# The second layer's norm and first value products beside the last accumulation; values, first gate tile, routing's transposes and level 0 moved by a chunk

## The chip, the cores and the metric

The kernel runs on one core of one Trainium2 chip. The metric is the device time of one execution in microseconds (us); the median of three runs of the kernel before is 2987.86 us (2985.18 to 2990.16).

## What is computed

A decoder trunk of two layers on 512 tokens of width 1024, in fp32:

```python
for i in range(DEPTH):                       # DEPTH = 2
    h = rmsnorm(x, norm_mix[i])
    proj = h @ w_in[i]                       # 1024 x 3088, split into three causal mixers
    o_da = diff_attention(q, k, v, ...)      # 4 heads
    o_sc = short_conv(sc_b, sc_c, sc_h, conv_w[i])
    o_g  = gla(g_q, g_k, g_v, log_a)         # gated linear attention, then norm and silu gate
    x = x + concat([o_da, o_sc, o_g]) @ w_out[i]
    x = x + peer(rmsnorm(x, norm_ffn[i]), w_q, keys1, keys2, u, v)   # 16384 experts, 8 heads, top 16
return rmsnorm(x, norm_final)
```

## The kernel before

Every product of two fp32 matrices is made of three matmuls on high and low parts (`mm3`: high by high, high by low, low by high, in the rows L79, L80 and L81). A part is split by a ScalarE cast (high) and a VectorE subtraction (low), in `split` (L84, L85) or in the like lines of the PEER stage.

A layer is one `mixer` and one `peer`. In `mixer`, the norm's generator `norm_T` takes the token blocks of 128 in the order 3, 0, 1, 2: normed rows on VectorE (L205), eight transposes on TensorE (psn, L209), high and low part out of PSUM (L211, L212). The columns of `w_in` come as slabs: `slab` loads four pieces of two k tiles (wraw, three buffers, L260) on the queue of SyncE (SP) and splits them. The first slab (column 2560) gives the values of the gated linear attention (psv), the next (column 2816, 272 wide) its output gate and low-rank decay (psp). Then `across` makes the other projections, and `fill` runs the generator `gla` between them up to a sum of costs; its first level (level 0) is the row pst (L589), which reads ks and qs from VectorE, and further on stand trk (transposes of kd) and psu.

`peer` treats all 16384 experts densely for tokens 0 to 383 (TD), in 128 chunks of 128 experts; tokens 384 to 511 get their 128 experts a token by indirect loads instead (`gathered`, side work on POOL and VectorE that `tick` hands out; it ends in yacc). For a chunk, `hidden` is 24 psh matmuls with the split u rows and a Gelu into ht; for the first 72 chunks (NPRE) ht is stored to H in DRAM. Meanwhile `routing` runs on VectorE: `route` makes the top 16 of a block and three transposes (rtr, L1109 to L1111) for one-hot lists, and `gate_matrix` turns them into one-hot rows (oha, ohb, ohh, ohl) and psg matmuls; the gates go to G in DRAM. After chunk 74 the second phase goes over the chunks, from 72 on and then 0 to 71: `w_hi` multiplies ht by the gate tile g, loaded from G for eight chunks at a time (`load_g`, L889), and casts it, `v_hi` casts the v rows (vraw, L884), `w_lo` and `v_lo` make the low parts, and `accumulate` is 18 pv matmuls into six PSUM banks. The last four chunks are accumulated as a group, block by block (`group`, 24 matmuls each of three blocks), and each block's x is added from PSUM (L1003), with its norm's factor made right after (`x_rstd`, L191, on ScalarE and small VectorE operations).

What sets the order: each engine runs its instructions in one order, SP's loads too. A scheduler sets it from the program's order and its own costs, except for instructions under `pin`/`keep_in_program_order`, which keep the program's. `issue_after` holds an instruction's place behind another. A tile waits for the readers of what had its memory before.

Of the kernel before, what the change touches and what calls it, by code (L numbers as in the profile page):

```python
# [7 lines left out]
F32 = mybir.dt.float32  # L8
F32R = mybir.dt.float32r
# [10 lines left out]
P = 128  # L20
# [47 lines left out]
class K:  # L68
# [152 lines left out]
    def mixer(self, L):  # L221
# [3 lines left out]
        with ExitStack() as mc:  # L225
# [3 lines left out]
            qT = mp.tile([P, 4, T], F32, name="qT")  # L229
            kT = mp.tile([P, 4, T], F32, name="kT")  # L230
            va = mp.tile([P, TB, T], F32, name="va")
            hh, hl = self.new_act()
            rows = lambda t: [t[:, 2 * i:2 * i + 2].rearrange("p a b -> p (a b)") for i in range(2)]
            norm = self.norm_T(ins["norm_mix"][L:L + 1, :], hh, hl, rows(va) + rows(kT), order=ORDER)
            with ExitStack() as wc:
                wp = wc.enter_context(tc.tile_pool(name="wpool", bufs=2, reuse_waits="tile"))
                qp = wc.enter_context(tc.tile_pool(name="qkn", bufs=2, reuse_waits="tile"))
# [56 lines left out]
                if L == 0:  # L294
                    self.constants(qT.rearrange("p a b -> p (a b)"), turn)
# [392 lines left out]
    def peer(self, L, xh, xl, rest):  # L688
# [3 lines left out]
        with ExitStack() as pc:  # L692
# [151 lines left out]
            ahead(0)  # L844
            best(NQ - 1)
            qc.close()
            with tc.tile_pool(name="route", bufs=1, reuse_waits="tile") as rp, tc.tile_pool(name="onehot", bufs=2, reuse_waits="tile") as hp:

                def routing():
                    for tb in range(TB):  # L850
                        if tb == ROUTE_AT:
                            yield from self.route(V12[3], I12[3], rp, gat, idx=idx, base=L * NCH * P)
                            yield None
                        if tb == TB - 1:
                            continue
                        gt = rp.tile([P, P], F32, tag="gt", name="gt")
                        yield from self.route(V12[tb], I12[tb], rp, gt, hk=(E1, E2, GH, GL), tb=tb)
                        for bt in range(P // TBAT):
                            yield from self.gate_matrix(tb * (P // TBAT) + bt, E1, E2, GH, GL, G, hp)

                work = routing()
                spent, live = 0.0, False
# [11 lines left out]
                for w in work:  # L874
                    print("leftover routing", w)
            lc.close()
            vp = pc.enter_context(tc.tile_pool(name="vstream", bufs=1, reuse_waits="tile"))
            late = vp
            pvs = [self.psA.tile([P, 512], F32, tag="a", name=f"pv{i}") for i in range(4)]
            pvs += [self.psC.tile([P, 512], F32, tag="c", name=f"pv{i}") for i in (4, 5)]  # L880
            order = list(range(NPRE, NCH)) + list(range(NPRE))
            def load_v(c):
                vs[c] = vp.tile([P, D], F32, tag="vraw", name="vraw", bufs=NVR)
                pin(nc.sync.dma_start(vs[c], ins["v_rows"][(L * NCH + c) * P:(L * NCH + c + 1) * P, :]))  # L884

            def load_g(c, h=None):
                if c // GE not in gt:
                    g = vp.tile([P, TD // TBAT, GE * TBAT], F32, tag="g", name="g", bufs=NG)
                    pin(nc.sync.dma_start(g, G[c // GE]))  # L889
                    gt[c // GE] = g  # L890
                if c < NPRE:
                    hs[c] = new_h() if h is None else h
                    pin(nc.sync.dma_start(hs[c], H[c]))

            vh, vl, wh, wl = {}, {}, {}, {}

# [21 lines left out]
                if i < NCH - NS:  # L918
                    f(order[i])

            ws, raws = [], {}

            def ahead_v(c):
                if not ws:
                    t = self.up.tile([P, 4, TD], F32R, tag="uwa", name="wsa", bufs=NUW // 2)
                    ws.extend([t[:, 0:2], t[:, 2:4], self.up.tile([P, 2, TD], F32R, tag="uraw", name="wsb", bufs=NUR)])
                t = self.up.tile([P, 2, D], F32R, tag="uwb" if len(raws) < 2 else "uwa", name="vs", bufs=NUW // 2)
                vh[c], vl[c] = t[:, 0], t[:, 1]
                t = ws.pop(0)
                wh[c], wl[c] = t[:, 0], t[:, 1]  # L930
                raws[c] = [self.up.tile([P, n], F32, tag="uraw", name=nm, bufs=NUR) for n, nm in ((D, "vr"), (TD, "hr"))]
# [32 lines left out]
            for i, c in enumerate(order):  # L964
                rate = RATE[1] if c >= NPRE else RATE[2]
                if i:
                    load_u(NPRE + i + LAG + 4)
                at(load_v, i + 3)
                at(load_g, i + 4)
                split_u(NPRE + i + LAG + 2)  # L970
                if i + LAG < NF:
                    hidden(order[i + LAG])
                tick(rate / 2)
                at(v_lo, i + 1)
                at(w_lo, i + 1)
                at(w_hi, i + 2)
                at(v_hi, i + 2)
                for k in range(NS):
                    j = NCH - 6 + 4 * (k - NS)
                    for step, f in ((j, ahead_v), (j + 2, ahead_hi), (j + 3, ahead_lo)):  # L980
                        if i == step:
                            f(order[NCH - NS + k])
                if i < NCH - NS - 1:
                    for tb in range(TD // P):
                        accumulate(tb, i)
                tick(rate / 2)
            for _ in side:
                pass
            nc.vector.tensor_tensor(self.x[:, 3], self.x[:, 3], yacc, op=OP.add)
# [4 lines left out]
            if last:  # L994
                fg = gp.tile([P, D], F32, tag="row", name="fg", bufs=NROW)
                nc.sync.dma_start(fg, ins["norm_final"].rearrange("(o d) -> o d", o=1).partition_broadcast(P))
                self.final(3, fg, gp)
            for tb in range(TD // P - last):
                for i in group:
                    accumulate(tb, i)  # L1000
# [3 lines left out]
                self.rstd[tb] = self.x_rstd(tb, sq)  # L1004
                if last:
                    self.final(tb, fg, gp)
            if last:
                tb = TD // P - 1
                y = gp.tile([P, D], F32, tag="row", name="fy", bufs=NROW)
# [28 lines left out]
    def route(self, V12, I12, rp, gate, hk=None, tb=0, idx=None, base=0):  # L1038
# [79 lines left out]
    def gate_matrix(self, bt, E1, E2, GH, GL, G, hp):  # L1118
        nc = self.nc
        stg = hp.tile([P, NCH, TBAT], F32, tag="stg", name="stg")  # L1120
        for o in range(TBAT // OHT):
# [10 lines left out]
            nc.vector.tensor_tensor(AH, A, tok(GH), op=OP.mult)  # L1132
            nc.vector.tensor_tensor(AL, A, tok(GL), op=OP.mult)
# [76 lines left out]
```

## Time and profile before

| | |
|---|---|
| median of three runs | 2987.86 us |
| profiled execution, its own time | 2988.17 us |
| its span, first to last instruction | 2986.4 us |
| VectorE busy | 80% |
| ScalarE busy | 42% |
| GpSimd (POOL) busy | 24% |
| DMA, mean over the span | 255 GB/s |

The span is what the trace holds; the profiled execution's own time is 1.8 us more. A row of the timeline gives start, duration, engine, line, operation and tiles; the bracket at its end is the engine's idle time before it and what ended it. `psn<-ident,kT` reads: the tile psn is written from ident and kT. PE is TensorE, PEld its weight loads, DVE VectorE, ACT ScalarE, SPq the issues of SyncE's queue.

### The profile page before, as it was taken

The page shows a single profiled execution, that of the slowest core. Times are in us where ns is not written, and L with a number is a line of the kernel's source. Part 1 is how long each engine was busy: PE and PEld are TensorE (multiplying, and loading weights), DVE is VectorE, ACT ScalarE, POOL GpSimd, SP SyncE. Part 2 cuts the span into 40 slices and gives each one's busy share as a digit, 9 for nine tenths or more (in the row PEclk, how much of TensorE's full clock was granted, in tenths as well). Part 3 has the DMA queues.
Part 4 walks back from the last instruction along what each step waited for, and adds up shares of the span by engine and source line. Part 5 has one row for each costly group of instructions (what it writes and reads, how often), then busy time and mean ns, then how long its engine had stood idle before and what let it go on. Part 6 is the DMA issues. An engine that isn't in the chain of part 4 may idle for free.

```text
span 2986.4 us, 44512 instructions
## 1 busy us (share of the span) xinstructions
PE 2937.2 (98%) x16262; PEld 2616.0 (88%) x16262; DVE 2393.9 (80%) x4754; ACT 1256.5 (42%) x1859; POOL 711.4 (24%) x617
## 2 busy tenths in 40 slices
PE   7999999999999999999989999999999999999998
PEld 6878899999899999888878688999999999988887
DVE  6676999976877788877866769999758777888778
ACT  5253355665333332333353433556553333323333
POOL 0200000222444455222102000012215444552220
PEclk9999999999999999999999999999999999999999
DMA  4322257999999998999543122579999999989995
GB/s 128 92 75 73 92 162 256 312 304 349 347 331 327 328 342 315 366 333 344 214 111 90 64 81 91 188 256 323 304 346 341 328 330 335 334 313 363 341 348 206
DMA packets 335867, 760.24 MB, mean 255 GB/s; under 512 B 30720, under 2 KB 191392, under 8 KB 331552
## 3 DMA queue, kind: packets, MB, share of 16 engines
q1 hardware_dynamic: 160656, 435.19, 40.8%
q0 software_dynamic: 75776, 271.62, 25.6%
q10 hardware_dynamic: 99216, 50.60, 5.6%
q8 instruction: 127, 2.08, 0.3%
q14 instruction: 92, 0.75, 0.1%
HBM read 673.15 MB, written 81.00 MB: 253 GB/s over the span
## 4 chain that ended last, share of the span: by engine, by line
PE 92%; DVE 4%; DMA 2%; ACT 1%; issue 1%; SPq 0%; ACTq 0%; DVEq 0%
PE pv L80 11%; PE pv L79 11%; PE pv L81 11%; PE psh L79 11%; PE psh L80 11%; PE psh L81 11%; PE psp L80 2%; PE psp L79 2%; PE psp L81 2%; PE psq L79 2%; PE psq L80 2%; PE psq L81 2%; PE psg L1139 2%; PE psg L1140 1%; PE pss L743 1%
## 5 line engine op out<-in xcount | busy, mean ns | idle before, releaser
L806 POOL DMA_INDIRECT row<-in_u_rows,idx x256 | 344.8, 1347 | 1358.7 <-DMA H<-ht 686.7
L79 PE MATMUL pv<-vh,wh 128*128 128x512 f32 x1500 | 583.0, 390 | 8.0 <-ACT vh L904 8.0
L80 PE MATMUL pv<-vl,wh 128*128 128x512 f32 x1500 | 584.7, 390 | 0.1
L81 PE MATMUL pv<-vh,wl 128*128 128x512 f32 x1500 | 583.8, 390 | 0.0
L806 POOL DMA_INDIRECT row<-in_v_rows,idx x256 | 315.3, 1232 | 597.4 <-DVE yacc L822 545.2
L724 ACT ACTIVATE ht<-psh 128x384 f32<-128x384 f32 x256 | 125.9, 492 | 775.7 <-PE psh L81 773.3
L899 DVE TENSOR_TENSOR vl<-vraw,vh 128x1024 fp32r<-128x1024 f32 x250 | 305.9, 1224 | 111.0 <-ACT vh L904 100.3
L79 PE MATMUL psh<-ahi,uwb 128*128 128x384 f32 x1024 | 348.2, 340 | 0.0
L79 PE MATMUL psh<-ahi,uwa 128*128 128x384 f32 x1024 | 346.4, 338 | 0.0
L80 PE MATMUL psh<-alo,uwb 128*128 128x384 f32 x1024 | 345.7, 338 | 0.0
L81 PE MATMUL psh<-ahi,uwb 128*128 128x384 f32 x1024 | 345.4, 337 | 0.0
L80 PE MATMUL psh<-alo,uwa 128*128 128x384 f32 x1024 | 344.2, 336 | 0.0
L81 PE MATMUL psh<-ahi,uwa 128*128 128x384 f32 x1024 | 344.1, 336 | 0.0
L79 PEld LDWEIGHTS pv<-vh,wh 128*128 128x128 f32 x1500 | 282.0, 188 | 63.2 <-ACT vh L904 8.6
L81 PEld LDWEIGHTS pv<-vh,wl 128*128 128x128 f32 x1500 | 282.3, 188 | 59.4 <-DVE wl L899 0.7
L80 PEld LDWEIGHTS pv<-vl,wh 128*128 128x128 f32 x1500 | 282.3, 188 | 56.0 <-DVE vl L899 1.6
L822 DVE SCALAR_TENSOR_TENSOR yacc<-row,wk,yacc 128x1024 f32<-128x1024 f32 x254 | 325.4, 1281 | 1.8
L912 ACT CAST wh<-ht 128x384 fp32r<-128x384 f32 x250 | 127.9, 512 | 432.8 <-DVE ht L1028 415.7
L813 DVE SCALAR_TENSOR_TENSOR row<-row,xg 128x1024 f32<-128x1024 f32 x256 | 308.7, 1221 | 0.0
L709 DVE TENSOR_TENSOR uwb<-uraw,uwb 128x1024 fp32r<-128x1024 f32 x144 | 176.0, 1222 | 123.3 <-ACT uwb L708 123.0
L709 DVE TENSOR_TENSOR uwa<-uraw,uwa 128x1024 fp32r<-128x1024 f32 x144 | 175.8, 1223 | 117.0 <-ACT uwa L708 116.8
L904 ACT CAST vh<-vraw 128x1024 fp32r<-128x1024 f32 x250 | 262.5, 1050 | 1.9 <-DMA vraw<-in_v_rows 1.9
(342 smaller groups left out, 5727.6 us busy)
## 6 DMA issues: line engine op xcount, KB each, us to landing
uraw<-in_peer_u SPq DMA_DIRECT2D x256, 512.0 KB, 5.4
vraw<-in_v_rows SPq DMA_DIRECT2D x250, 512.0 KB, 6.6
G<-stg ACTq DMA_DIRECT2D x48, 1024.0 KB, 7.5
g<-G SPq DMA_DIRECT2D x32, 1536.0 KB, 10.2
H<-ht SPq DMA_DIRECT2D x144, 192.0 KB, 4.8
ht<-H SPq DMA_DIRECT2D x138, 192.0 KB, 7.4
wraw<-in_w_in SPq DMA_DIRECT2D x88, 256.0 KB, 3.0
uraw<-in_peer_w_q SPq DMA_DIRECT2D x32, 512.0 KB, 3.4
```

The lines of the kernel that those rows point to most:

```text
L79: mm(ps, ah, bh, start=first, stop=False)
L80: mm(ps, ah, bl, start=False, stop=False)
L81: mm(ps, al, bh, start=False, stop=last)
L709: self.last = pin(nc.vector.tensor_tensor(lo, src, hi.bitcast(F32), op=OP.subtract))
L724: pin(nc.scalar.activation(hs[c], ps, AF.Gelu))
L806: nc.gpsimd.indirect_dma_start(out=r, out_offset=None, in_=ins[name], in_offset=bass.IndirectOffsetOnAxis(ap=idx[:, k:k + 1], axis=0))
L813: nc.vector.scalar_tensor_tensor(r, r, 1.0, xg, op0=OP.mult, op1=OP.mult, accum_out=hd[:, k:k + 1])
L822: nc.vector.scalar_tensor_tensor(yacc, r, wk[:, k:k + 1], yacc, op0=OP.mult, op1=OP.add)
L899: self.last = pin(nc.vector.tensor_tensor(lo, src, hi.bitcast(F32), op=OP.subtract))
L904: pin(nc.scalar.copy(vh[c], vs[c]))
L912: pin(nc.scalar.copy(wh[c], hs[c]))
L1139: nc.tensor.matmul(ps[:, j], B[at], AH[at], start=True, stop=False)
```

## The change

1. *Between the layers.* In layer 0's `peer`, the first slab of layer 1 (`first`) is loaded six chunks before the end, split before the last group, and `norm_T` of layer 1 runs between the group's blocks; the psv products follow in the same place (`values`), into PSUM tiles that layer 1's `mixer` copies out. Layer 0's own start stays.
2. *Level 0.* `fill(10)` is called after the first copy of the next projection, not ahead of it.
3. *Routing.* `route` and `gate_matrix` yield once more for the first block, and the loop leaves off for that chunk at such a yield: the transposes and the first one-hot row move back by a chunk.
4. *First values and gate tile.* The pool of the second phase is opened when routing ends; the first v load is issued in chunk 71's step and the first g load in chunk 72's, ahead of the remaining u loads.
5. The buffers of the last three chunks (`ahead_v`) are other ones: vraw, ht, g, uraw, uwa and xg in place of uwa, uwb and uraw. Not shown below.

```diff
-            hh, hl = self.new_act()
-            rows = lambda t: [t[:, 2 * i:2 * i + 2].rearrange("p a b -> p (a b)") for i in range(2)]
-            norm = self.norm_T(ins["norm_mix"][L:L + 1, :], hh, hl, rows(va) + rows(kT), order=ORDER)
+            if L == 0:
+                hh, hl = self.new_act()
+                rows = lambda t: [t[:, 2 * i:2 * i + 2].rearrange("p a b -> p (a b)") for i in range(2)]
+                norm = self.norm_T(ins["norm_mix"][L:L + 1, :], hh, hl, rows(va) + rows(kT), order=ORDER)
+            else:
+                hh, hl = self.hh, self.hl
...
-                next(norm)
-                wh, wl = slab(2560, 256)
+                if L == 0:
+                    next(norm)
+                    wh, wl = slab(2560, 256)
                 for i, tb in enumerate(ORDER):
-                    next(norm, None)
-                    ps = self.psC.tile([P, 256], F32, tag="c", name="psv")
-                    for k in range(KD):
-                        self.mm3(ps, hh[:, k, tb * P:tb * P + P], hl[:, k, tb * P:tb * P + P], wh[:, k], wl[:, k],
-                                 k == 0, k == KD - 1)
+                    if L:
+                        ps = self.psv.pop(tb)
+                    else:
+                        next(norm, None)
+                        ps = self.psC.tile([P, 256], F32, tag="c", name="psv")
...
-                fill(10)
...
                         nc.scalar.copy(dst[:, 2 * h + j], ps)
+                        if i == j == 0:
+                            fill(10)
...
-                for c in range(NPRE + LAG):
-                    if c:
-                        ahead(c)
-                    if live:
-                        tick(RATE[0])
-                    while spent < DVE_STEP * (c + 1):
-                        w = next(work, 1e9)
-                        if w is None:
-                            live = True
-                        else:
-                            spent += w
...
+            for c in range(NPRE + LAG):
+                if c:
+                    ahead(c)
+                if live:
+                    tick(RATE[0])
+                while vp is None and spent < DVE_STEP * (c + 1):
+                    w = next(work, Ellipsis)
+                    if w is Ellipsis:
+                        rc.close()
+                        lc.close()
+                        vp = late = pc.enter_context(tc.tile_pool(name="vstream", bufs=1, reuse_waits="tile"))
+                    elif w is None:
+                        live = True
+                    elif w == 0.0:
+                        break
+                    else:
+                        spent += w
+                if c == NPRE - 1:
+                    load_v(order[0])
+                if c == NPRE:
+                    load_g(order[0])
...
-            with tc.issue_after(self.fetch.ins):
-                for i in range(4):
-                    if i < 3:
-                        at(load_v, i)
-                    at(load_g, i)
+            for i in range(1, 4):
+                at(load_g, i)
+                if i < 3:
+                    at(load_v, i)
...
+                if i == NCH - 6 and L < DEPTH - 1:
+                    first = self.up.tile([P, KD, 256], F32, tag="uwa", name="first", bufs=NUW // 2)
+                    for kh in range(0, KD, 4):
+                        pin(nc.sync.dma_start(first[:, kh:kh + 4], ins["w_in"][L + 1].rearrange(
+                            "(k p) c -> p k c", p=P)[:, kh:kh + 4, 2560:2816]))
...
+            else:
+                rows = [gp.tile([P, D], F32, tag="row", name=n, bufs=NROW) for n in ("grow", "xn")]
+                rows.insert(1, None)
+                self.hh, self.hl = self.new_act()
+                norm = self.norm_T(ins["norm_mix"][L + 1:L + 2, :], self.hh, self.hl, rows, order=ORDER)
+                next(norm)
+                sh, sl = ([vp.tile([P, KD // 2, 256], F32R, tag="vraw", name=n, bufs=NVR) for _ in range(2)] for n in ("slh", "sll"))
+                for j in range(4):
+                    ks = slice(j % 2 * 2, j % 2 * 2 + 2)
+                    self.split(sh[j // 2][:, ks], sl[j // 2][:, ks], first[:, 2 * j:2 * j + 2])
+                self.psv = {}
+
+                def values(j, tb):
+                    if j % 2 == 0:
+                        pair = self.psA.tile([P, 2, 256], F32, tag="a", name="psv")
+                        self.psv[tb], self.psv[ORDER[j + 1]] = pair[:, 0], pair[:, 1]
+                    t = slice(tb * P, tb * P + P)
+                    for k in range(KD):
+                        self.mm3(self.psv[tb], self.hh[:, k, t], self.hl[:, k, t], sh[k // 4][:, k % 4], sl[k // 4][:, k % 4],
+                                 k == 0, k == KD - 1)
+
             for tb in range(TD // P - last):
                 for i in group:
                     accumulate(tb, i)
@@ -1004,6 +1054,11 @@
                 self.rstd[tb] = self.x_rstd(tb, sq)
                 if last:
                     self.final(tb, fg, gp)
+                else:
+                    next(norm)
+                    if tb == TD // P - 1:
+                        for j, t in enumerate(ORDER):
+                            values(j, t)
...
+        if tb == 0:
+            yield 0.0
         E1, E2, GH, GL = hk
...
             yield 4.6
+            if bt == 0:
+                yield 0.0
```

SP's queue at the end of the first phase of layer 0 (uraw are the u rows, vraw the v rows, ht the hidden values stored to H), before:

```order
L705 DMA uraw<-in_peer_u 128x1024
L841 DMA H<-ht 128x384
L705 DMA uraw<-in_peer_u 128x1024 x3
L884 DMA vraw<-in_v_rows 128x1024
L889 DMA g<-G 128x3072
L884 DMA vraw<-in_v_rows 128x1024 x3
L705 DMA uraw<-in_peer_u 128x1024
```

and of the change:

```order
L849 DMA H<-ht 128x384
L713 DMA uraw<-in_peer_u 128x1024
L849 DMA H<-ht 128x384
L876 DMA vraw<-in_v_rows 128x1024
L713 DMA uraw<-in_peer_u 128x1024
L849 DMA H<-ht 128x384
L881 DMA g<-G 128x3072
L713 DMA uraw<-in_peer_u 128x1024 x3
L876 DMA vraw<-in_v_rows 128x1024 x3
```

The v load moved ahead of the last u load but three, and g from behind three u loads and a v load to right behind the last H store.

SP's queue between the layers, before (va and grow receive the norm's gain, turn the rotary tables, wraw the slabs):

```order
L199 DMA va<-in_norm_mix 128x1024
L300 DMA dgain<-in_diff_norm 128x1
L260 DMA wraw<-in_w_in 128x2x256 x3
L297 DMA turn<-turnd 64x1024
L299 DMA lamv<-in_lam_q 128x64
L260 DMA wraw<-in_w_in 128x2x256
L299 DMA lamv<-in_lam_k 128x64
```

and of the change:

```order
L1014 DMA first<-in_w_in 128x4x256 x2
L199 DMA grow<-in_norm_mix 128x1024
L307 DMA dgain<-in_diff_norm 128x1
L383 DMA cw<-in_conv_w 128x6
L304 DMA turn<-turnd 64x1024
L263 DMA wraw<-in_w_in 128x2x272 x4
L306 DMA lamv<-in_lam_q 128x64
```

The first slab (128x2x256) is now loaded as `first`, ahead of the gain. The next slab's four pieces (128x2x272) stand right behind turn, and turn shares its memory with the rows of the norm (grow and xn).

TensorE at the last accumulation of layer 0, before:

```order
L80 MATMUL pv_7847<-vs,wsb 128x512
L81 MATMUL pv_7847<-vs,wsb 128x512
L209 MATMUL psn<-ident,kT 128x128 x8
L79 MATMUL psv<-wh,ahi 128x256
L80 MATMUL psv<-wl,ahi 128x256
L209 MATMUL psn<-ident,kT 128x128 x4
L81 MATMUL psv<-wh,alo 128x256
```

and of the change, at the third of the four blocks' transposes:

```order
L81 MATMUL pv_7850<-gs 128x512
L79 MATMUL pv_7851<-gs 128x512
L209 MATMUL psn<-ident,xn 128x128 x8
L80 MATMUL pv_7851<-gs 128x512
L81 MATMUL pv_7851<-gs 128x512
L79 MATMUL psv<-slh,ahi 128x256
```

The psn of block 3 now stand behind 31 of the last 72 pv matmuls, those of block 0 behind 51, of block 1 behind 70 and of block 2 behind 47 of the 96 psv.

TensorE at the routing's transposes of layer 0, before:

```order
L81 MATMUL psh<-ahi,uwb 128x384
L1109 MATMUL rtr_4003<-ident,ex 128x128
L79 MATMUL psh<-ahi,uwb 128x384
L80 MATMUL psh<-alo,uwb 128x384
L81 MATMUL psh<-ahi,uwb 128x384
L79 MATMUL psh<-ahi,uwb 128x384
L1110 MATMUL rtr_4003<-ident,ex 128x128
L1111 MATMUL rtr_4003<-ident,gt 128x128
L80 MATMUL psh<-alo,uwb 128x384
L81 MATMUL psh<-ahi,uwb 128x384
```

and of the change:

```order
L81 MATMUL psh<-ahi,uwb 128x384
L79 MATMUL psh<-ahi,uwb 128x384
L80 MATMUL psh<-alo,uwb 128x384
L81 MATMUL psh<-ahi,uwb 128x384
L1166 MATMUL rtr_4036<-ident,ex 128x128
L1167 MATMUL rtr_4036<-ident,ex 128x128
L1168 MATMUL rtr_4036<-ident,gt 128x128
L79 MATMUL psh<-ahi,uwa 128x384
L80 MATMUL psh<-alo,uwa 128x384
```

The three transposes stand together, the first of them 24 psh further back, the other two 20; the first psg follow 48 psh behind them.

More of the change, by code (lines that the diff above doesn't have):

```diff
@@ L283, in down @@
                         yield slice(2 * pr, 2 * pr + 2), ps
-                next(norm)
-                wh, wl = slab(2560, 256)
+                if L == 0:
+                    next(norm)
+                    wh, wl = slab(2560, 256)
                 for i, tb in enumerate(ORDER):
-                    next(norm, None)
-                    ps = self.psC.tile([P, 256], F32, tag="c", name="psv")
-                    for k in range(KD):
-                        self.mm3(ps, hh[:, k, tb * P:tb * P + P], hl[:, k, tb * P:tb * P + P], wh[:, k], wl[:, k],
-                                 k == 0, k == KD - 1)
+                    if L:
[4 more added lines that the diff above has]
+                        for k in range(KD):
+                            self.mm3(ps, hh[:, k, tb * P:tb * P + P], hl[:, k, tb * P:tb * P + P], wh[:, k], wl[:, k],
+                                     k == 0, k == KD - 1)
                     nc.scalar.copy(gv[:, tb], ps)
@@ L846, in peer @@
             qc.close()
[L847 to L862, printed above, removed]
-                for c in range(NPRE + LAG):
-                    if c:
-                        ahead(c)
-                    if live:
-                        tick(RATE[0])
-                    while spent < DVE_STEP * (c + 1):
-                        w = next(work, 1e9)
-                        if w is None:
-                            live = True
-                        else:
-                            spent += w
-                for w in work:
-                    print("leftover routing", w)
@@ L876, in peer @@
[L876 to L880, printed above, removed]
+            rc = pc.enter_context(ExitStack())
+            rp = rc.enter_context(tc.tile_pool(name="route", bufs=1, reuse_waits="tile"))
+            hp = rc.enter_context(tc.tile_pool(name="onehot", bufs=2, reuse_waits="tile"))
@@ new lines, in routing @@
+            def routing():
+                for tb in range(TB):
+                    if tb == ROUTE_AT:
+                        yield from self.route(V12[3], I12[3], rp, gat, idx=idx, base=L * NCH * P)
+                        yield None
+                    if tb == TB - 1:
+                        continue
+                    gt = rp.tile([P, P], F32, tag="gt", name="gt")
+                    yield from self.route(V12[tb], I12[tb], rp, gt, hk=(E1, E2, GH, GL), tb=tb)
+                    for bt in range(P // TBAT):
+                        yield from self.gate_matrix(tb * (P // TBAT) + bt, E1, E2, GH, GL, G, hp)
@@ L881, in peer @@
             order = list(range(NPRE, NCH)) + list(range(NPRE))
+            vp = None
             def load_v(c):
@@ L893, in load_g @@
                     pin(nc.sync.dma_start(hs[c], H[c]))
+            work = routing()
+            spent, live = 0.0, False
+            for c in range(NPRE + LAG):
[19 more added lines that the diff above has]
+                    load_g(order[0])
+            assert vp is not None
+            pvs = [self.psA.tile([P, 512], F32, tag="a", name=f"pv{i}") for i in range(4)]
+            pvs += [self.psC.tile([P, 512], F32, tag="c", name=f"pv{i}") for i in (4, 5)]
             vh, vl, wh, wl = {}, {}, {}, {}
@@ L919, in at @@
                     f(order[i])
-            ws, raws = [], {}
+            raws = {}
             def ahead_v(c):
[L924 to L931, printed above, removed]
+                k = len(raws)
+                new = lambda n, tag, bufs, pool=vp: pool.tile([P, n], F32R, tag=tag, name=tag + "s", bufs=bufs)
+                if k == 0:
+                    t = self.up.tile([P, 2, D], F32R, tag="uwa", name="vs", bufs=NUW // 2)
+                    vh[c], vl[c] = t[:, 0], t[:, 1]
+                elif k == 1:
+                    vh[c], vl[c] = (new(D, "uraw", NUR, self.up) for _ in range(2))
+                else:
+                    t = new(2 * D + 2 * TD, "g", NG)
+                    vh[c], vl[c], wh[c], wl[c] = t[:, 0:D], t[:, D:2 * D], t[:, 2 * D:2 * D + TD], t[:, 2 * D + TD:]
+                if k < 2:
+                    t = new(2 * TD, "uraw", NUR, self.up) if k == 0 else new(2 * TD, "xg", 1, pp)
+                    wh[c], wl[c] = t[:, 0:TD], t[:, TD:]
+                raws[c] = [vp.tile([P, D], F32, tag="vraw", name="vraw", bufs=NVR), new_h()]
                 pin(nc.sync.dma_start(raws[c][0], ins["v_rows"][(L * NCH + c) * P:(L * NCH + c + 1) * P, :]))
@@ L997, in peer @@
                 self.final(3, fg, gp)
+            else:
[14 more added lines that the diff above has]
+                    t = slice(tb * P, tb * P + P)
+                    for k in range(KD):
+                        self.mm3(self.psv[tb], self.hh[:, k, t], self.hl[:, k, t], sh[k // 4][:, k % 4], sl[k // 4][:, k % 4],
+                                 k == 0, k == KD - 1)
             for tb in range(TD // P - last):
@@ L1006, in peer @@
                     self.final(tb, fg, gp)
+                else:
+                    next(norm)
+                    if tb == TD // P - 1:
+                        for j, t in enumerate(ORDER):
+                            values(j, t)
             if last:
```

## The prediction

> **What bounds the kernel now.** I read the page first (share of the span by engine), then the waits of TensorE, then the granted clock in windows around each wait, then the timeline there.
>
> ```profile
> PE 2937.2 (98%) x16262; PEld 2616.0 (88%) x16262; DVE 2393.9 (80%) x4754; ACT 1256.5 (42%) x1859; POOL 711.4 (24%) x617
> ```
> TensorE (PE) is busy for 2937.2 of 2986.4 us. The change keeps its matmuls, so only idle time, or matmuls that run slowly, can give anything. The idle time is 49.2 us, and the waits view names its releasers:
>
> ```profile
> PE psn L209 <- DMA lamv<-in_lam_q: 13.6, 1, 13.6
> PE pv L79 <- ACT vh L904: 8.0, 2, 4.7
> PE psn L209 <- DVE kT L205: 5.5, 1, 5.5
> PE rtr L1110 <- DVE ex L1083: 4.7, 2, 2.4
> PE pst L589 <- DVE ks L580: 4.0, 2, 2.0
> PE pss L475 <- ACT e L482: 2.8, 2, 1.4
> ```
> Columns: total us, times, longest. 13.6 is the start of the kernel, which the change leaves. Four kinds remain that it touches: 8.0 at the first pv of each layer, 5.5 between the layers, 4.7 at the routing's transposes, 4.0 at level 0; pss stays. Bare, that is 22.2 us. But a wait costs more than itself. The windows view has us, the engines' busy time and then the granted clock (after POOL), around one wait of each kind and over a stretch without any:
>
> ```profile
> 58.00:68.00 10.00, 7.99 (x28) 6.20 (x28) 8.56 (x13) 3.96 (x9) 0.00 (x0) 0.83 0.20 54
> 200.00:206.00 6.00, 4.56 (x18) 2.22 (x17) 5.59 (x13) 4.07 (x10) 0.00 (x0) 1.00 0.01 1
> 408.00:418.00 10.00, 7.64 (x37) 7.29 (x36) 10.00 (x26) 2.04 (x5) 0.00 (x0) 0.83 0.41 140
> 750.00:760.00 10.00, 6.72 (x24) 5.37 (x24) 7.00 (x10) 4.15 (x6) 1.64 (x1) 0.83 0.61 231
> 800.00:1490.00 690.00, 689.95 (x3305) 603.87 (x3305) 557.47 (x705) 239.99 (x338) 255.17 (x210) 1.00 0.88 325
> 1496.00:1506.00 10.00, 7.08 (x31) 6.27 (x32) 8.23 (x12) 4.52 (x8) 0.00 (x0) 0.52 0.67 190
> ```
> Without waits the clock is 1.00 for 690 us. Around the waits of level 0 (58 to 68), routing (408 to 418) and first pv (750 to 760) it is 0.83 over 10 us: 10 x 0.17 = **1.7 us** lost beside each wait. The pss wait of 1.4 us (200 to 206) lost none. So a wait of 2.0 us or more costs itself and 1.7 us, one of 1.4 us only itself.
>
> Here a rule speaks against counting that way. The Trainium skill ("TensorE: Matmul & The Clock Gate", "What's actually happening") says the clock halves after at least one idle window of about 3.4 us. By it the waits of 2.0 and 2.4 us would cost no clock, and my sum would be 4 x 1.7 = 6.8 us smaller; the 0.83 at 58 and 408 disagrees, so I go by the rows.
>
> **The change part by part.** The sum is made against the profiled execution, 2988.17 us (span 2986.4 and 1.8 around it), 0.3 above the median of 2987.86.
>
> *Between the layers.*
>
> ```profile
> 1489.64 0.39 PE L81 MATMUL pv<-vs,wsa 128*128 128x512 f32 x1
> 1492.36 0.39 PE L81 MATMUL pv<-vs,wsb 128*128 128x512 f32 x1
> 1498.23 1.97 PE L209 MATMUL psn<-ident,kT 128*128 128x128 f32 x8 [5.48 <-DVE kT L205]
> 1505.67 0.28 PE L79 MATMUL psv<-wh,ahi 128*128 128x256 f32 x1
> 1517.04 0.28 PE L79 MATMUL psp<-wh,ahi 128*128 128x272 f32 x1
> ```
> Start, duration. 1505.67 to 1517.04 holds 84 psv matmuls and 16 psn transposes, 11.37 us at full rate, 0.114 each. The 13.31 us before it, from the last pv, hold one pv (0.23: twelve take 2.72 from 1489.64), 16 psn and 12 psv, which at that rate are 0.23 + 28 x 0.114 = 3.4. Excess: **9.9 us** of wait and half rate. The change puts the norm's psn between the pv and the psv, so it can all go. What is late next is the norm itself:
>
> ```profile
> 1476.30:1492.50 16.20, 16.20 (x73) 13.30 (x71) 8.16 (x28) 3.46 (x6) 1.86 (x2) 1.00 0.01 2
> 1492.11 1.37 DVE L1003 TENSOR_TENSOR x<-x,pv 128x512 f32<-128x512 f32 x2 [1.36 <-PE pv L81]
> 1496.89 2.48 DVE L205 SCALAR_TENSOR_TENSOR kT<-x,ry,va 128x1024 f32<-128x1024 f32 x2 [0.70 <-DMA va<-in_norm_mix]
> L84 ACT CAST wh<-wraw x96: 602/620/669, 12.3 to 1656.0; 128x512 fp32r<-128x512 f32 x88, 128x544 fp32r<-128x544 f32 x8
> L85 DVE TENSOR_TENSOR wl<-wraw,wh x96: 665/691/736, 14.6 to 1659.6; 128x512 fp32r<-128x512 f32 x88, 128x544 fp32r<-128x544 f32 x8
> ```
> Last pv to psn took 5.87 us, 0.70 of it for the gain's row; without it 5.2. The order leaves between a token block's last pv and its psn 27 and 22 pv (6.1 and 5.0 us) and 47 psv (5.4 us): all within half a microsecond or so of enough, with other work in the way. VectorE does 8.16 us in the 16.2 us of the last group; added are 4 low parts of the slab (4 x 0.69), 4 normed blocks (4 x 1.24) and the low parts of three of them (6 x 0.69): 8.16 + 11.9 = 20 us in some 22 up to the last psn. So VectorE is nearly full, and each of four psn waits a little: I take 1.4 us in all, between 0 (the chain fits) and 4 (a queue of one slab piece and one normed block, 1.9, behind two of them). None reaches 2 us, so no half rate. The ScalarE casts (4 x 0.62) fit in its idle 12.7 us. The two 512 KB loads of `first` come six chunks earlier, behind the last value loads on SP's queue, and replace four piecewise loads: nothing waits for them.
>
> Second, the next slab. Its four loads now stand on SP's queue behind the load of `turn`, whose buffer is that of the norm's rows: it waits for the last psn.
>
> ```profile
> 1493.68 1.58 SPq L260 DMA_DIRECT2D wraw<-in_w_in  x3
> 1495.43 0.46 SPq L297 DMA_DIRECT2D turn<-turnd  x1
> 1498.60 0.62 ACT L84 CAST wh<-wraw 128x512 fp32r<-128x512 f32 x1 [3.88 <-DMA wraw<-in_w_in]
> DMA to landing us min/median/max: 2.6/3.0/8.7
> ```
> After the last psn stand 49 psv, 5.6 us (49 x 0.114). `turn` takes 0.5 to issue, a piece 3.0 (median) to land, 0.6 and 0.7 to split: first piece ready at 4.9. The fourth waits for the first's buffer (three of them), so its high half is there at 4.9 + 3.0 + 0.6 = 8.5 and its low half at 9.2; PE wants it 18 matmuls into the slab, at 5.6 + 18 x 0.12 = 7.8. Wait: **1.3 us**; with landings of 2.6, 0.5; of 4.9 (1493.68 to 1498.60), 1.3 + 2 x 1.9 = 5.1 and then 1.7 of clock. I take 1.3, since 3.0 is the median. Place: 9.9 - 1.4 - 1.3 = **7.2** (9.4 with both at their low ends, 0.8 below nothing with both at their high ends and the clock).
>
> *Level 0.* The fill is called after the first copy of the next projection, so 16 matmuls of 0.23 (3.6 us) stand ahead of pst; ks still comes when it came. 3.6 is more than 2.0: the wait closes in layer 0, 2.0 + 1.7. In layer 1 the decay chain (az) has three slab casts among its steps on ScalarE where it had one, which makes it 1 to 1.3 us later, so 0.5 is left (0 to 1.3). The psp matmuls that now run before pst are missing behind it, ahead of trk, whose input kd was ready with ks: hidden. 3.7 + 3.2 = **6.9** (6 to 7.4).
>
> *Routing's transposes.*
>
> ```profile
> 413.10 0.33 PE L1110 MATMUL rtr<-ident,ex 128*128 128x128 f32 x1 [2.36 <-DVE ex L1083]
> 413.35 0.32 DVE L1032 MAX8 sv<-cand 128x8 f32<-128x50 f32 x2
> 414.14 1.21 DVE L709 TENSOR_TENSOR uwb<-uraw,uwb 128x1024 fp32r<-128x1024 f32 x1
> 418.88 1.22 DVE L1133 TENSOR_TENSOR ohl<-oha,GL 128x2048 f16<-128x2048 f16 x1
> ```
> PE was free from 410.74. The waiting transpose moves 20 psh behind, at 4.16 us a chunk of 24 (below) 3.5 us, more than 2.36: closed in both layers, 4.7 + 2 x 1.7 = 8.1. Next are the first psg, 48 psh (8.3 us) behind the transposes, at 422.5. They need ohl, which ended at 420.1; now twenty small operations of the next block's top-16 stand before the one-hot row on VectorE, 0.16 each (five begin from 413.35 to 414.14): 420.1 + 3.2 = 423.3. I take a wait of 0.7 in each layer (0 to 1.9). **6.7** (4.3 to 8.1).
>
> *First gate tile.*
>
> ```profile
> 727.83 0.33 SPq L841 DMA_DIRECT2D H<-ht  x1
> 731.99 0.33 SPq L841 DMA_DIRECT2D H<-ht  x1
> 741.33 0.57 SPq L889 DMA_DIRECT2D g<-G  x1
> 751.29 1.03 DVE L1028 TENSOR_TENSOR ht<-ht,g 128x384 f32<-128x384 f32 x2 [10.44 <-DMA g<-G]
> 753.44 1.87 PE L79 MATMUL pv<-vh,wh 128*128 128x512 f32 x6 [3.28 <-ACT vh L904]
> g<-G SPq DMA_DIRECT2D x32, 1536.0 KB, 10.2
> ```
> H leaves once in a chunk: 4.16 us. The load of g moves on SP from behind three u loads to right behind the last H: issue at 732.4 in place of 741.3, landing with 10.2 at 742.6. The work from landing to pv was 2.2 us; it now queues with chunk 74's cast and splits, and I put the low halves at 747.6. PE was idle from 750.16 and reaches pv 12 psh (2.1 us) earlier, at 748.1: margin 0.5. Both waits (8.0) and their clock (3.4) go: **11.4**. With a landing of 11.9, the longest of these loads, 1.2 is left in each layer: 9.0. The v load and u76 change places, u77 to u79 stand behind g; they feed chunks that PE reaches 8 us and more after 750, against landings of 5.4: hidden. If the cover fails, one chunk waits up to 4 us, once a layer.
>
> Sum: 7.2 + 6.9 + 6.7 + 11.4 = 32.2. 2988.2 - 32.2 = 2956.0, in terms of the median 2955.7: **2956 us**.
>
> **The rivals.**
> 1. *The slab behind `turn` takes the removed wait's place.* For it: SP's queue is in order, `turn` is held by the last psn, and landings of 4.9 occur there. Against: the loads of 1493.68 competed with the norm's row and `turn`; the median is 3.0. Price: 5.1 + 1.7 - 1.3 = 5.5 more: 2961.
> 2. *All new waits vanish* (VectorE reorders better than I estimate, landings of 2.6): 1.4 + 0.8 + 0.5 + 1.4 = 4.1 less: 2952.
> 3. *The gate tile isn't earlier*: that part does not do what it says, because g must wait for the last store of G. That store was issued at 722 by the trace and such stores land in 7.5 (page), before 732, so I think little of it. Price 11.4: 2967.
> 4. *Several small waits each lose the clock.* Between 1.4 and 2.0 us no row tells whether the clock halves, and I leave four waits of 0.5 to 1.3 and the run of psn waits, 1.4 in sum. Against: the stretch at 200, 1.4 in one piece, kept 1.00. If four of them do lose it, 4 x 1.7 = 6.8: 2963. The Trainium skill (page and section above) calls its window of about 3.4 us free-running, so that the place of an idle stretch would count as well as its length.
> 5. *Slower: the chip withholds clock from a PE that never rests.* One mechanism, over the whole span: the seven waits of 2 us and more between start and end are its rests now. With 2956 us of work, a mean clock that falls by 1.1% gives all of it back, and by 1.3% the kernel is slower by 0.2%: 2994. Against: 690 us with 689.95 busy at 1.00.
>
> **How the numbers follow.** Forecast 0.5; rival 1 0.15; rival 2 0.12; rival 3 0.06; rival 4 0.1; rival 5 0.03; 0.04 for what I haven't seen. The range runs from 2949 (rival 2 less 3, half the spread of the three runs, 2985.18 to 2990.16) to 2968 (rival 3, or rival 1 with both gate tiles late and psg at its high end); outside lie rival 5, what I haven't seen, and cases that add up. A difference of 0.2% (6 us) is about what a measurement of this kernel can tell from none: faster by more 0.91, within 0.05, slower 0.04.
>
> **What would show it.** In the waits: no pv, rtr or pst row of 2 us or more; psn with about 1.4 in all; one psp row of about 1.3 at the first 272-wide matmul, released by wl or wh. In the windows: 1.00 around those four places. SP's timeline: g issued about 732 and `turn` right after the last psn. The idle total should be about 31 us, of which 13.6 at the start and 8 at the end. I am wrong if a wait of over 2 us stands at the slab, at psg or at a first pv, or if the clock is under 1.00 without a wait.

## The result and the profile after

The changed kernel takes 2963.0 us (median of 6 runs, 2960.48 to 2964.56), the one before 2984.9 in the same comparison: ratio 0.9927, 95% interval 0.9916 to 0.9938. The forecast was 2956, the range 2949 to 2968. The gain is 22 us where 32 were forecast: the way is right, the time lies inside the range, 7 us above the forecast.

The page and the waits of TensorE after (total us, times, longest):

```profile
PE 2927.0 (99%) x16262; PEld 2605.3 (88%) x16262; DVE 2392.4 (81%) x4754; ACT 1258.2 (42%) x1860; POOL 719.1 (24%) x617
...
PE psn L209 <- DMA lamv<-in_lam_q: 13.8, 1, 13.8
PE pss L483 <- ACT e L490: 2.8, 2, 1.4
PE pv L80 <- DVE vl L918: 2.4, 3, 1.2
PE psg L1199 <- DVE ohl L1190: 1.0, 2, 0.5
PE psu L635 <- ACT kdT L627: 0.9, 1, 0.9
PE psh L81 <- DVE uwa L717: 0.8, 2, 0.4
PE psu L635 <- DVE S L637: 0.7, 2, 0.4
PE psn L209 <- DVE xn L205: 0.6, 2, 0.3
```
The four kinds of wait that the change aimed at are gone (pv for vh, psn for kT between the layers, rtr, pst); the 13.8 at the start and pss stay. New are short ones, 1.2 us at most. The windows at the four places, granted clock behind POOL's busy time:

```profile
58.00:68.00 10.00, 10.00 (x46) 8.30 (x45) 9.89 (x17) 5.23 (x10) 0.00 (x0) 1.00 0.37 107
404.00:414.00 10.00, 10.00 (x61) 9.96 (x60) 10.00 (x49) 3.36 (x7) 0.00 (x0) 1.00 0.61 194
740.00:750.00 10.00, 10.00 (x52) 8.79 (x51) 3.48 (x4) 3.20 (x5) 0.00 (x0) 1.00 0.66 261
1485.00:1495.00 10.00, 9.41 (x78) 9.12 (x78) 6.28 (x16) 3.30 (x6) 0.00 (x0) 1.00 0.01 2
```
The clock is 1.00 at all of them. Where the 24.7 us between the two profiled executions (2988.17 and 2963.48) come from is seen by the starts of the same matmuls in the timelines, in us from one to the other (`psp 101 to 300`: from the start of the psp matmul numbered 101 to that of the one numbered 300, counted from 0 over both layers):

```
stretch (from, to)                           before  again(e5)  after   gain  forecast
level 0, layer 0 (psp 101 to 300)             62.88   61.22     59.52   3.4   3.7
level 0, layer 1 (psp 800 to 1000)            63.13   63.00     60.43   2.7   3.2
routing, layer 0 (psh 0 to 1000)             200.43  198.87    197.90   2.5   3.35
routing, layer 1 (psh 3072 to 4072)          200.43  200.43    197.91   2.5   3.35
first pv, layer 0 (psh 1700 to 1900)          56.22   56.47     53.23   3.0   5.0
first pv, layer 1 (psh 4772 to 4972)          57.59   57.91     51.93   5.7   6.4
between the layers (pv 2200 to psp 800)       69.26   69.00     62.60   6.7   7.2
end (pv 4304 to the last, and from it on)     76.9    77.5      79.3   -2.4   0
```
Start-up and the rest give 0.7.

### The profile page after: what moved, and what is told of

Read it like the earlier page. It is cut to its first block, busy times and chain, and to the rows that moved or that the text cites. A ratio compares the mean times of both kernels' runs of the same rounds, so it can differ in the third digit from the quotient of the medians.

```text
span 2961.7 us, 44532 instructions
## 1 busy us (share of the span) xinstructions
PE 2927.0 (99%) x16262; PEld 2605.3 (88%) x16262; DVE 2392.4 (81%) x4754; ACT 1258.2 (42%) x1860; POOL 719.1 (24%) x617
## 4 chain that ended last, share of the span: by engine, by line
PE 87%; DVE 8%; DMA 2%; ACT 2%; issue 1%; SPq 0%; DVEq 0%; ACTq 0%
PE pv L80 11%; PE pv L81 11%; PE pv L79 11%; PE psh L79 10%; PE psh L81 10%; PE psh L80 10%; PE psp L80 2%; PE psp L81 2%; PE psp L79 2%; PE psq L79 2%; PE psq L80 2%; PE psq L81 2%; PE psg L1198 1%; PE psg L1199 1%; PE pss L751 1%
## 5 line engine op out<-in xcount | busy, mean ns | idle before, releaser
L814 POOL DMA_INDIRECT row<-in_u_rows,idx x256 | 351.5, 1373 | 1338.0 <-DVE row L821 627.4
L923 ACT CAST vh<-vraw 128x1024 fp32r<-128x1024 f32 x250 | 262.5, 1050 | 15.5 <-DMA vraw<-in_v_rows 11.4
```

The costliest lines, as they stand in the source:

```text
L814: nc.gpsimd.indirect_dma_start(out=r, out_offset=None, in_=ins[name], in_offset=bass.IndirectOffsetOnAxis(ap=idx[:, k:k + 1], axis=0))
L923: pin(nc.scalar.copy(vh[c], vs[c]))
```

## The experiments

**e5, the kernel before, profiled again.** No edit.

> The kernel before, unchanged, profiled once more. The six halved-clock stretches of its first profile begin at multiples of 3.413 us of one phase, and in the earlier runs of this study waits of 2.35 and 2.01 us kept the clock at 1.00. Theory A (the clock is halved for one window of 3.413 us where the window before it was idle for more than some 1.8 us; the windows run free, with a phase drawn at the start): at another phase at least one of the four waits of 2.0 to 2.4 us keeps 1.00, by the phase some half of them; the waits themselves stay at 2.0, 2.4, 3.3, 4.7 and 5.5. Each that keeps it is 1.7 us. All halved stretches again have one phase. Rival B (a wait of 2.0 or more halves the clock whatever its place): all seven are halved again.

This one execution took 2984.16 us. (The first profile has seven halved stretches, as the end of the expectation counts them, not six.) The windows of this execution at level 0, routing, level 0 of layer 1 and its routing:

```profile
57.00:67.00 10.00, 7.99 (x36) 6.36 (x35) 9.98 (x17) 5.06 (x10) 0.00 (x0) 1.00 0.33 96
406.00:416.00 10.00, 7.64 (x46) 7.29 (x45) 10.00 (x27) 3.47 (x7) 0.00 (x0) 1.00 0.41 144
1537.00:1547.00 10.00, 7.99 (x28) 6.14 (x27) 8.25 (x14) 4.57 (x10) 0.00 (x0) 0.83 0.18 52
1888.00:1898.00 10.00, 7.65 (x37) 7.29 (x36) 10.00 (x26) 2.04 (x5) 0.00 (x0) 0.83 0.40 129
```
The waits are the same 2.0 and 2.4 us; in layer 0 they kept 1.00, in layer 1 they didn't. The trace's clock records tell why (start of each halved stretch up to the last matmul, its length, and the rest that its start leaves when divided by 3.4133 us):

```
before, first profile               before again (e5)
  61.81   3.41  rest 0.37              749.69   3.41  rest 2.17
 413.38   3.41  rest 0.37             1493.79   6.83  rest 2.17
 754.71   3.41  rest 0.37             1541.58   3.41  rest 2.17
1495.40  10.24  rest 0.38             1893.15   3.41  rest 2.17
1546.61   3.41  rest 0.38             2234.48   3.41  rest 2.17
1898.18   3.41  rest 0.38
2239.51   3.41  rest 0.39
```
Windows of 3.41 us follow each other with one phase for an execution, and a window is run at half clock when TensorE was idle long enough in the one before it: 1.99 us or more did it in the first profile, 1.81 and 1.87 did not in e5. Over the profiles of all runs here, every window at full clock with 1.95 us of idle time or more was followed by a halved one, and none with 1.66 or less; in between both occurred (1.75 in e7 and 1.89 in e4 did it; 1.77 in e3, 1.87 in e5 and 1.89 in e9 and e12 did not), so the border is not sharp. Once halved, less keeps it so: 0.70 us in the first profile (window from 1498.82) and 1.19 in e5 (from 1493.79) did, 0.55 in e6 (from 1488.54) and less did not. Theory A holds and rival B falls; two halvings missed make e5's two stretches of layer 0 1.6 us shorter each (table).

**e1, the second chunk's v load early, and e2, own buffers for the last raw v rows.** Edits (the first two pieces are e1's, the others e2's):

```diff
                 if c == NPRE:
                     load_g(order[0])
+                    load_v(order[1])
...
-                if i < 3:
+                if i == 2:
                     at(load_v, i)
...
-                    vh[c], vl[c] = (new(D, "uraw", NUR, self.up) for _ in range(2))
+                    t = self.up.tile([P, 2, D], F32R, tag="uwb", name="vs", bufs=NUW // 2)
...
-                raws[c] = [vp.tile([P, D], F32, tag="vraw", name="vraw", bufs=NVR), new_h()]
+                raws[c] = [self.up.tile([P, D], F32, tag="uraw", name="vr", bufs=NUR), new_h()]
```

> The changed kernel with one load moved: the second chunk's v rows are loaded right behind the first gate tile, ahead of three u loads, in place of behind them. Theory A (the second chunk's values land late, its cast holds ScalarE's queue, its low half comes late, and TensorE pays more than the idle time it shows): the waits of pv for vl at the second chunk, 1.24 us in layer 0 and 0.37 in layer 1, go, and with them the slow matmuls beside them, 1.8 and 0.9 us by the timeline; about 2.7 us faster than the changed kernel, 2960. Rival B (VectorE's queue, where a u split and a gathered row stand ahead of that low half, sets it): the wait stays over 0.5 us and the time stays at 2963. Rival C (the u loads, now later, starve a psh chunk): a new wait of psh for uwa or uwb in the next four chunks, 1 us or more.

> The changed kernel with the last three chunks' raw v rows in buffers of their own (those of the u rows), in place of a slot each in the ring of four that the running v rows use. Theory A (each of these loads takes a slot for three steps, so the running loads come a chunk later and a landing of 5.7 us is not covered): the pv wait of 0.76 us late in layer 1 goes, and 1.3 us with the matmuls beside it, 2961.7. Rival B (one late landing by chance, whatever the buffers): the wait is gone or there at random, also in layer 0, and the v loads are issued when they were.

In the changed kernel's timeline the second chunk goes like this:

```profile
733.49 1.37 SPq L876 DMA_DIRECT2D vraw<-in_v_rows  x3
746.19 1.05 ACT L923 CAST vh<-vraw 128x1024 fp32r<-128x1024 f32 x1 [5.38 <-DMA vraw<-in_v_rows]
750.14 0.40 PE L79 MATMUL pv<-vh,wh 128*128 128x512 f32 x1
750.50 1.22 DVE L918 TENSOR_TENSOR vl<-vraw,vh 128x1024 fp32r<-128x1024 f32 x1
751.78 0.50 PE L80 MATMUL pv<-vl,wh 128*128 128x512 f32 x1 [1.24 <-DVE vl L918]
752.59 0.40 PE L79 MATMUL pv<-vh,wh 128*128 128x512 f32 x1
```
The load leaves 6.3 us after g's (727.23), behind three u loads; ScalarE waits 5.38 us for it, with a u cast behind. From 750.14 to 752.59 three matmuls take 2.45 in place of 0.68 us: the wait of 1.24 cost 1.8. With e1 the two stretches of the first pv fall from 53.23 and 51.93 to 52.09 and 51.01, 2.1 us; both second-chunk waits are gone, one of 0.5 is left at the first chunk, and no psh starves. Median 2960.5 (ratio 0.9921, 0.9901 to 0.9941). Theory A by the timeline, somewhat smaller; by the times alone e1 can't be told from the changed kernel, since the intervals overlap. In e2 (2961.0; 0.9912, 0.9895 to 0.9929) the late pv wait of 0.76 in layer 1 is gone, but so it is in e1, e3, e4, e6, e8 and e10, which don't have that edit (e7 has one of 0.36 there): my theory fell. A late landing in that execution fits (rival B); what made it late was not followed.

**e3, routing back, and e4, level 0 back.** Edits, e3's first:

```diff
-        if tb == 0:
-            yield 0.0
...
-            if bt == 0:
-                yield 0.0
```

```diff
+                fill(10)
                 for i in range(4):
...
-                        if i == j == 0:
-                            fill(10)
```

> The changed kernel with the routing's part undone: no extra yields. Theory A (that part was worth 2.5 us a layer, since VectorE, full there, gives 1.5 us of the 4.1 back as waits of psg for ohl and of a later psh for uwa): rtr waits of about 2.4 us come back, psg and uwa waits go, the clock there is 0.8 again; 5 us slower than the changed kernel, 2968. Rival B (the psg and uwa waits belong to other parts): the time rises by 8, to 2971, and the uwa waits stay.

> The changed kernel with level 0 filled ahead of the next projection again. Theory A (worth 3.4 in layer 0 and 2.8 in layer 1 net of new psu waits): pst waits of 2.0 come back, 6.2 us slower than the changed kernel, 2969; the psu waits of 0.35, 0.87 and 0.35 go. Rival B (the psu waits of layer 1 come from the changed slab order between the layers, not from level 0): they stay and the time rises by 7.4.

e3: 2962.25 (0.9917, 0.9901 to 0.9934), no slower; the times of both theories (2968 and 2971) missed. Its profiled execution is the slowest of the four (2967.1). In it, at routing of layer 0 and of layer 1:

```profile
404.00:414.00 10.00, 7.65 (x46) 7.30 (x45) 10.00 (x26) 3.36 (x7) 0.00 (x0) 1.00 0.37 128
1877.00:1887.00 10.00, 7.67 (x37) 7.32 (x36) 10.00 (x26) 2.04 (x5) 0.00 (x0) 0.83 0.38 128
```
The waits (2.35 and 2.33) are back, one halved, the other not. The stretches are 199.3 and 201.1, 4.6 us over the changed kernel's, which is theory A's size; the psg waits of 0.5 and the uwa waits of 0.4 go, and psh waits of 0.3 and 0.2 stand at other chunks, so part of what TensorE gains by the moved transposes is handed back. That this is because VectorE is busy for all of the 10 us is argued, not shown. Why the median does not show the 4.6 us is open. e4: 2968.5 (0.9938, 0.9922 to 0.9955), 5.5 slower than the changed kernel; pst waits 2.01 (clock 1.00) and 2.33 (0.83), stretches 61.2 and 63.3, and no psu waits of over 0.3: theory A. But the two stretches make 4.5 us, and the profile has another loss, at the first pv of layer 1, where the stretch is 56.27 in place of 51.93 and the clock was halved from 2217.13:

```profile
2216.26 0.50 PE L79 MATMUL pv<-vh,wh 128*128 128x512 f32 x1 [1.53 <-ACT vh L922]
2217.52 0.80 PE L80 MATMUL pv<-vl,wh 128*128 128x512 f32 x1 [0.76 <-DVE vl L917]
```
The wait for the first gate tile's chunk thus comes back in some executions: besides e4 it stands in layer 0 of e3 (1.67 and 0.76, halved, stretch 55.89) and of e6 (1.10 and 0.76, stretch 54.13). The edits of e4 and e6 lie elsewhere, e3's in the routing ahead of it. In layer 0, g was issued at 730.82 in e6 and between 725.4 and 727.6 in the changed kernel, e1, e2, e4, e10 and e11; what delays it was not followed. So the closed gap has little to spare, as the prediction's margin of 0.5 us said.

**e6, between the layers back, the changed buffers kept, and e9, the buffers alone:** the kernel before with the change's `ahead_v`. e6's edit, beside the removal of `values` and the norm from `peer`:

```diff
-            if L == 0:
+            if True:
                 hh, hl = self.new_act()
...
-                if i == NCH - 6 and L < DEPTH - 1:
+                if False:
```

> The changed kernel with the part between the layers undone: no early slab, the norm and the value products in layer 1's own start. Theory A (worth 8.3 us up to the next slab, 1.6 lost again in the next slab's and the projection's first part): 6 to 7 us slower than the changed kernel, 2969 to 2970, with a psn wait of 5.5 and a clock under 0.6 over 10 us. Rival B (what the slab behind the rotary table's load costs is as large as what is gained): under 2 us.

> The kernel before with one part of the change alone: the buffers of the last three chunks of each layer are the changed ones. Theory A (with them the memory of the norm's gain row is free before the last pv matmuls end, so its load and the slab's no longer follow them; this part, which the prediction left out, carries half of what the place between the layers gives): the gain row is issued 2 to 3 us ahead of the last pv's end in place of at it, the psn wait there is about 3.4 in place of 5.5 us, the stretch from the last chunks to the 272-wide slab 3.5 us shorter than before; time 3 to 4 us under before. Rival B (the early norm and value products carry it all): psn wait of 5.5, the time that of before within 1 us.

e6: 2964.4 (0.9926, 0.9909 to 0.9942), only 1.4 slower. Theory A missed: the psn wait is 3.4, not 5.5. The time is one that rival B allowed (under 2 us), but not for its reason: the stretch between the layers is 65.8 us, up to the next slab 4.8 longer than the changed kernel's, the slab and the projection behind it only 1.6 shorter. The gain row's load (L199) is issued 2.7 us before e6's last pv ended:

```profile
1482.31 0.33 SPq L199 DMA_DIRECT2D va<-in_norm_mix  x1
...
1488.40 0.81 PE L209 MATMUL psn<-ident,kT 128*128 128x128 f32 x3 [3.40 <-DVE kT L205]
```
In the kernel before, whose last pv started at 1492.36, it was issued as that ended; in e9, whose last pv started at 1493.84, ahead of that (the first row is that of the kernel before, the others are e9's):

```profile
1492.78 0.33 SPq L199 DMA_DIRECT2D va<-in_norm_mix  x1
...
1491.54 0.33 SPq L199 DMA_DIRECT2D va<-in_norm_mix  x1
...
1497.63 1.09 PE L209 MATMUL psn<-ident,kT 128*128 128x128 f32 x8 [3.40 <-DVE ry L175]
```
So e9 shows that the buffers do this by themselves: theory A. The stretch between the layers is 65.8 us (before 69.26, changed 62.60), the median 2980.9 (11 runs; 0.9985, 0.9976 to 0.9993). Of the 6.7 us there 3.5 are the buffers', and 3.2 the early norm and products add to them; what these would give without the buffers was not run.

**e7, the first loads back** behind the u loads:

```diff
-                if c == NPRE - 1:
-                    load_v(order[0])
-                if c == NPRE:
-                    load_g(order[0])
...
-            for i in range(1, 4):
-                at(load_g, i)
-                if i < 3:
-                    at(load_v, i)
+            with tc.issue_after(self.fetch.ins):
+                for i in range(4):
+                    if i < 3:
+                        at(load_v, i)
+                    at(load_g, i)
```

> The changed kernel with the first value and gate loads at their old place on SP's queue, behind three u loads. Theory A (worth 3.0 in layer 0 and 5.7 in layer 1 by the landmarks): waits of over 3 us at the first pv of both layers, clock 0.83 there, 8 to 9 us slower than the changed kernel, 2971 to 2972; the second chunk's wait for vl is gone. Rival B (the moved transposes and the earlier TensorE alone set the margin): under 4 us.

2969.1 (0.9942, 0.9926 to 0.9959), 6.1 slower. Waits at the first pv 3.8 and 1.75, both halved; stretches 56.67 and 54.67, 6.2 us over the changed kernel's. The mechanism is A's, the size between the two theories'; why layer 1 waits for less than the 4.7 of before was not followed.

**e8, lighter routing**, with e1's edit:

```diff
-DVE_STEP = 2.72
+DVE_STEP = 2.64
```

> The kernel of e1 (second v load early) with VectorE's routing work handed out at 2.64 in place of 2.72 us of it a chunk. Theory A (VectorE is the bound of the routing stretch, so TensorE's gain there comes back as waits for it): the uwa waits of 0.37 and 0.39 and the psg waits of 0.46 fall, 1 to 2 us faster than e1 over the two layers. Rival B (where single instructions stand sets these waits, not the load): they move or stay, the time within 1 us of e1; a later end of routing costs up to 1 us at the first gate tile.

2978.2 (0.9968, 0.9956 to 0.9981): both theories' times are wrong. In its waits

```profile
PE psg L1199 <- DVE ohh L1190: 8.3, 2, 4.2
PE pv L79 <- ACT vh L924: 6.9, 2, 3.8
```
the psg wait for a whole chunk (4.2 us, halved as well): the first one-hot row starts 6.1 us later on VectorE than in e1 (420.12 for 413.99), while TensorE reaches the psg 1.4 us later (at 419.5 for 418.15). Routing ends later too, and g is issued at 740.65 in place of e1's 725.41, and the first pv waits again (3.8 us at the most). Whether less load on VectorE would help is left open by it.

**e10, the change again; e11, e1 and e2 together; e12, e11 with routing back.**

> The changed kernel once more, on the chip of e11 and e12, so that they can be compared. 2960.5 to 2964.6 before. Theory A (no wait in it fills half of a window of 3.413 us, so its phase does not matter): runs within 5 us of each other, where those of before spread over 10 or more; the pv wait of 0.76 us late in layer 1 is absent (chance) or there (its buffers).

> The changed kernel with the edits of e1 and e2 together: second v load early, own buffers for the last raw v rows. Theory A: 2 to 3 us faster than e10, all of it from the second chunk's pv. Rival B: the medians of e10 and e11 within 1 us.

> e11 with the routing's part undone. Theory A (the part takes away an rtr wait of 2.35 us in each layer, which halves the clock in some two executions of three, and adds 1.0 at psg and at uwa): 3 to 6 us slower than e11, with more spread. Rival B (VectorE, full there, gives all of it back, as e3's median equal to the changed kernel's lets one think): within 1.5 us of e11.

e10: 2962.1, five runs over 5.3 us (0.9926, 0.9913 to 0.9939); the 17 of before that it is compared with spread over 12.0. e11: 2959.3 (0.9925, 0.9911 to 0.9939); its first-pv stretches are 51.01 in both layers, 3.5 us under e10's 53.88 and 51.63, but two of five runs (2964.9, 2967.0) leave the ratios alike, so the better version is shown by the timeline and not by the times. (Start-up alone, up to psp 101, took between 46.4 and 48.1 us in the profiles here, so that a gain of a us or two is better read from stretches.) e12: 2964.6 (0.9937, 0.9922 to 0.9951), six runs over 12.6 us; routing's stretches 4.0 us over e11's, with the clock halved at one of the two rtr waits. Theory A for e10, e11 and e12, by the timelines; the intervals of e10, e11 and e12 overlap.

## Why the prediction was right in direction and 7 us off

- *What bounds the kernel*: right. TensorE's waits were the whole of it, and all four kinds closed. The stretches where a wait was closed give some 26.5 of the 32.2 us, and the end takes 2.4 back.
- *"A wait of 2.0 us or more costs itself and 1.7 us"*: wrong as a rule. It costs 1.7 more if some 1.9 us of it fall into one window of 3.41 us (e5, e3). The first profile's phase was one at which every wait did, which was luck. Its 2988.17 lies 2.2 us above the median of the 17 later runs, 2985.95, and 3.3 above the 2984.9 of the result; that much of the forecast gain was not in the median. How much of it is the halvings' is not shown: e5, with two fewer, is 4.0 us below the first profile, 1.3 of it at the start. The time after does not hang on this, since no stretch between start-up and the last matmul was halved there. The prediction quoted the Trainium skill ("TensorE: Matmul & The Clock Gate", "What's actually happening") for an idle window of about 3.4 us and set it aside. On the length the rows were right: 1.95 us in one window always was enough here. On the window that runs free, which stood there only beside rival 4, the Trainium skill was right: the common rests of 0.37 and of 2.17 agree.
- *First gate tile, 11.4*: measured 8.7. The step "the v load and u76 change places, u77 to u79 stand behind g ... hidden" looked at the first chunk's v and the u loads. The second chunk's v load stood behind these too, and the closed gap brought its pv forward; moving it gave 2.1 us back (e1). With e1's and e2's edits together the place gives 11.8 (e11: 51.01 in both layers).
- *Routing, 6.7*: measured 5.1. psg waited 0.5 as priced (0.7); the uwa waits of 0.4 were not seen, though VectorE's 10.00 of 10 us, a reason to look for them, stood in the quoted row of 408. In the changed kernel's timeline such a wait costs 0.7, the two matmuls from 509.69 to 510.71 taking 1.02 in place of 0.35 us:

```profile
509.69 0.34 PE L80 MATMUL psh<-alo,uwa 128*128 128x384 f32 x1
510.43 0.44 PE L81 MATMUL psh<-ahi,uwa 128*128 128x384 f32 x1 [0.40 <-DVE uwa L717]
510.71 0.34 PE L79 MATMUL psh<-ahi,uwa 128*128 128x384 f32 x1
```
- *Short waits at their idle time*: too cheap. 1.24 us cost 1.8 and 0.40 cost 0.7.
- *Level 0, 6.9*: 6.1; the new waits came at psu, behind the place that was priced.
- *Between the layers, 7.2*: 6.7, the size right, half of the way to it wrong. The slab wait was 0.4, not 1.3, and the psn waits 0.6, not 1.4, but the next slab and projection run 1.6 longer (22.84 for 21.24), and half of the gain is the buffers' (e9), whose effect on the gain row's load I had left out. That the sum came so near is luck.
- *End*: 2.4 lost, put at nothing in the forecast. 1.3 of it stand at a late landing that six of the seven other profiles without e2's edit lack; the last 1.1, behind the last matmul, was not followed.
- *Rivals*: the slab behind `turn` (1), the gate tile (3) and the chip's clock (5) did not come, and the new waits did not all vanish (2). Rival 4 gave 2963, the measured time, but its halvings at short waits did not come (1.4 and 1.24 us kept 1.00).

## What to carry to other kernels

Before a wait is priced by one profile, look whether the clock's halved stretches have a common phase: a wait of about the border's length costs its surplus in some executions only, and the median holds a share of it. When a wait is closed, go through what the next chunk needs as well, since it too is wanted that much earlier; and follow the memory of every buffer that a change renames to the loads that wait for it.

## What the runs showed of the hardware

In these profiles the granted clock fell to one half for a whole window of 3.41 us after every window with 1.95 us or more of idle TensorE, and after none with 1.66 or less; once halved it stayed so after 0.70 us of idle time and came back after 0.55 or less. The windows run on with one phase through an execution (rest 0.37 to 0.39 at all seven places of the first profile, 2.17 at all five of e5).
